# A two-layer decoder step on one core: the last squares on TensorE, two query blocks in one visit, stored keys and values claimed apart

## The chip, the core and the metric

The kernel runs on one core of one Trainium2 chip. The metric is the device time of one execution, in microseconds (us), as a median over runs. A core has TensorE (PE; its weight loads are listed apart as PEld), VectorE (DVE), ScalarE (ACT), GpSimd (POOL) and SyncE (SP), which here only issues transfers. Each engine works through its own instructions in the order of the program. TensorE's clock is granted at one of two levels, 2.4 GHz (1.00 in the tables) or 1.2 GHz (0.50).

## What is computed

One step of a two-layer trunk on 1056 tokens: 1024 of a prompt and 32 of a sample group (8 sequences of 4). All of it is fp32, with a model width of 1024. In short form:

```python
# layer 0: one projection feeds a convolution branch and a dilated attention branch
h = rms_norm(x, pre_norm[0])                 # mean of squares over the 1024 channels
a_val, a_gate, a_out, q, k, v, b_gate = split(h @ w_in_ab)      # 7 blocks of 1024
ya = swish(layer_norm(conv31(a_val * sigmoid(a_gate)))) * silu(a_out)
q, k = rope(q), rope(k)                      # 16 heads of 64
# same heads under (window, dilation) (128,1), (512,4), (2048,16), merged by their denominators
yb = merged_attention(q, k, v) * silu(b_gate)
#   sample group: its keys and values are the stored caches (2048 rows) and its own 4
x1 = x + rms_norm(concat(ya, yb) @ w_out_ab, post_norm[0])
# layer 1: gated linear recurrence, 16 heads of 128 x 128
q, f, v, g = split(rms_norm(x1, pre_norm[1]) @ w_in_c)
y = x1 + rms_norm(recurrence(q, f, v) * silu(g) @ w_out_c, post_norm[1])
```

The outputs are y, the new keys and values, the new convolution rows and the new states.

## The kernel before

**The dense stream.** Tokens lie along the free axis in three chunks of 384, 384 and 288 columns. A dense job is one block of 128 output channels: for each chunk, 8 x 3 matmuls of 128 x 128 weights in the split form (high and low halves in fp32r). There are 152 such jobs: 56 for the first projection, 16 for each output projection, 64 for layer 1. They are one long stream on TensorE, and everything else is side work.

**The order.** `Kern` is a planner that runs while the program is built. It keeps a clock per engine (`account`, with the costs in `cost` and `array`), and it writes every instruction in the order in which it decides. After each three dense matmuls it calls `sides()`, which places the next step (`Atom`) of any thread whose inputs are due by its books. A step for TensorE is placed once its inputs have been due for 300 ns (`LEAD`) and the clocks of ACT and DVE are at most 1500 ns ahead. Threads go by priority. All transfers are issued by SP, in the planner's order. The chip then follows that fixed order, and each engine waits at its next instruction for whatever is late.

**Memory.** `Arena` has 28 pages of 1056 columns, 17 halves of 512 and 8 small buffers. A thread may claim pages for what it will take (`claim`, in pages and halves); a step with a claim isn't placed until that many are free. PSUM has three buffers for the dense stream (d), four for the side work (x, taken by `px()`) and one for attention outputs (o).

**Prologue.** X is loaded as four tiles per chunk, each holding two blocks of channels side by side. ScalarE squares them. VectorE adds tile 1 to tile 0, 3 to 2, 2 to 0, and folds the two halves of tile 0 into one (`add`, `fold`). `stat(c)` multiplies the result with a constant matrix (`self.ones`), which sums over partitions, and `rstd_of` makes the factors of the norm. The evacuations of the first dense job are placed once the statistic of chunk 2 is due. `turn(c)` scales the tables of the rotation on POOL.

**Attention of the prompt.** There are eight pairs of heads, each a thread (`attention`). The prompt is cut into eight query blocks of 128. `qk(i)` writes the scores of block i for both heads in the 64 x 32 tiling of TensorE: 8 matmuls on the near keys and, from block 2 on, 8 on the far keys. VectorE adds the mask and takes the extremum, and ScalarE takes the exponential. `tr(i)` and `far(i)` turn the probabilities, and `pv(i)` and `far_pv` multiply them with the values. Such a group of matmuls, placed between dense ones, is called a visit here. In the trace one fp32 matmul is two records.

**Stored-key rounds.** For the sample group there are 16 rounds (8 pairs, two groups g of four sequences), each a thread made by `dec_thread` from `dec_round`. A round issues four loads of keys (kc) and four of values (vc), builds the query block, writes the scores (`qk`), turns the probabilities (`tr1`, `tr2`), multiplies them with the values (`pv`) and stores its part (`out`). The rounds run beside the last 16 jobs of the first projection and the first of the output projection.

Of the kernel before, what the change touches and what calls it, by code (L numbers as in the profile page):

```python
# [177 lines left out]
class Kern:  # L178
# [481 lines left out]
    def prologue(self):  # L660
# [50 lines left out]
        def add(c, k, m, eng):  # L711
            x, y = X[c, k], X[c, m]
            do(lambda: eng.tensor_tensor(x.f, x.f, y.f, op=OP.add), ("s", c, k), ("s", c, k), ("s", c, m))
            y.free()
# [6 lines left out]
        def stat(c):  # L721
            def f():
                w = CW[c]
                x = X[c, 0]
                p = self.px()
                nc.tensor.matmul(p[:, :w], self.ones.f, x[:, :w], start=True, stop=True)
                self.rstd_of(self.R[:, C0[c]:C0[c] + w], p[:, :w])
                x.free()
            return f
# [44 lines left out]
        for c in range(3):  # L774
            for k in range(n):
                square(c, k, True)
            add(c, 0, 1, V)
            add(c, 2, 3, V)
            add(c, 0, 2, V)
            fold(c)  # L780
        for c in range(3):
            self.fin["pro", c] = at["s", c, 0]
            self.spawn(f"pro{c}", 0.1 * c, [Atom(stat(c), "pe", [("pro", c)], ("r0", c)),
                                            Atom(turn(c), "pool", None, ("cs", c))])
# [170 lines left out]
    def attention(self, pr):  # L955
# [7 lines left out]
        def qk(i):  # L963
            def f():
                if i == 0:
                    S["den"] = A.alloc(16)
                    S["o"] = A.alloc(T)
                nf, nn = width(i)
                W = nf + nn
                kc = slice(128 * (i + 1) - nn, 128 * (i + 1))  # L970
                hs = [slice(64 * h, 64 * h + 64) for h in range(2)]
                ss = []
                for h in range(2):
                    P[i, h] = A.alloc(W + 8)
                    ss.append(self.px())
                q, k = S["q"], S["k"]
                for a, b, ks in ((nf, W, kc), (0, nf, None)):
                    for r in range(4):
                        for h in range(2):
                            if b > a:  # L980
                                nc.tensor.matmul(ss[h][32 * r:32 * r + 32, a:b],
                                                 q[hs[h], 128 * i + 32 * r:128 * i + 32 * r + 32],
                                                 k[hs[h], ks or slice(r, 128 * i, 4)], start=True, stop=True,
                                                 skip_group_check=True, tile_position=(64 * h, 32 * r))
                t = self.cur
                for h in range(2):
                    e = P[i, h]
                    m = e[:, W:W + 1]
                    self.resume(t)
                    nc.vector.tensor_tensor_reduce(e[:, :W], ss[h][:, :W], self.mask[:, NMASK - W:NMASK],  # L990
                                                   op0=OP.add, op1=OP.min, scale=-0.125, scalar=1e30, accum_out=m)
                    nc.scalar.activation(e[:, :W], e[:, :W], AF.Exp, scale=-1.0, bias=m,
                                         accum_out=S["den"][:, h * 8 + i:h * 8 + i + 1])
            return f
# [81 lines left out]
        for i in range(9):  # L1076
            if i < 8:
                atoms.append(Atom(qk(i), "pe", [K("pv", i - 2)] if i > 1 else [("ko", pr)], K("qk", i),
                                  (2, 7) if i == 0 else None))
# [310 lines left out]
    def dec_thread(self, pr):  # L1390
        nc, A = self.nc, self.A
        KN = NCK + NS
        for g in range(2):
            self.spawn(f"dec{pr}.{g}", 3 + 0.01 * (2 * pr + g), self.dec_round(pr, g, {}), ("att", pr))
# [18 lines left out]

    def dec_round(self, pr, g, R):
        nc, A = self.nc, self.A
        KN = NCK + NS

        def load(name, j):
            def f():
                b = A.alloc(NCK)  # L1420
                R.setdefault(name, []).append(b)
                nc.sync.dma_start(b.f, self.io[name][pr, 4 * g + j])
            return f
# [11 lines left out]
        def qk():  # L1435
# [22 lines left out]
            nc.scalar.activation(e[:, :KN], e[:, :KN], AF.Exp, scale=-1.0, bias=x[:, 2:3], accum_out=x[:, 3:4])  # L1458
            nc.vector.reciprocal(x[:, 4:5], x[:, 3:4])
# [38 lines left out]
        def out():  # L1498
# [3 lines left out]
            for h in range(2):  # L1502
# [6 lines left out]
        lds = [Atom(load(n, j), "sp", [], K(k) if j == 3 else None, (8, 0) if (k, j) == ("k", 0) else None, True)  # L1509
               for n, k in (("kc", "k"), ("vc", "v")) for j in range(4)]  # L1510
        return lds[:1] + [Atom(blk, "pool", [], K("q"))] + lds[1:] + ([Atom(lambda: self.dec_v(pr), "pe", [])] if g == 0 else []) + [
                Atom(qk, "pe", [K("k"), K("q")], K("s"), (6, 0)), Atom(tr1, "pe", [K("s")], K("t1")),
                Atom(tr2, "pe", [K("s")], K("t2")), Atom(pv, "pe", [K("t1"), K("t2"), K("v")], K("pv")),
                Atom(out, "pe", None, K("o"))]
# [1121 lines left out]
```

## Time and profile before

| | |
|---|---|
| median of 3 runs | 2325.9 us (2324.64 to 2326.06) |
| profiled execution | 2328.87 us |
| its span, first to last instruction | 2327.0 us, mean granted clock 0.994 |
| PE and PEld busy | 2262.7 and 2116.6 us (97% and 91%) |
| DVE, ACT, POOL busy | 1601.6, 1026.3, 1026.5 us (69%, 44%, 44%) |
| moved by DMA | 271.60 MB, 117 GB/s over the span |

All times in the profile are counted from the start of the span. Nearly every instruction is issued through one helper, so all rows carry its line, L158, and they are told apart by the names of the tiles: d, x and o are PSUM buffers, c are constants and the split X, b is any buffer of the arena, and kc, vc, wab and so on are arrays in device memory. A row "out<-in" gives what an instruction writes and reads, with the forms of both. The ends of matmuls are modelled, so what a group of them took is read from its start to the start of the next row.

### The profile page before, as it was taken

What the parts mean: (1) busy time and instruction counts of PE and PEld (TensorE: products, weight loads), DVE (VectorE), ACT (ScalarE), POOL (GpSimd) and SP (SyncE); (2) the same over time, 40 slices, a digit from 0 to 9 for tenths busy, and PEclk for the clock granted to TensorE, in tenths of its full rate; (3) what the DMA queues carried; (4) which work ended last, traced back from release to release, by engine and by line L of the source; (5) the groups of instructions that cost most, each with busy time, mean ns of one, the idle gap of its engine ahead of it and who ended that gap; (6) DMA issues with size and microseconds to landing.
All of it is one profiled execution on the core that took longest, in us unless ns stands there. A gap on an engine that the chain in (4) does not pass through costs nothing.

```text
span 2327.0 us, 42803 instructions
## 1 busy us (share of the span) xinstructions
PE 2262.7 (97%) x17415; PEld 2116.6 (91%) x17415; DVE 1601.6 (69%) x2477; ACT 1026.3 (44%) x1862; POOL 1026.5 (44%) x678
## 2 busy tenths in 40 slices
PE   7999999999999999999999999999999999999997
PEld 7988888888887788899989999999999999998997
DVE  7999899898996557533865666666766666667436
ACT  5454444444444322332564444444454444454422
POOL 4554474645555423543633333333333333344435
PEclk9999999999999999999999999999999999999999
DMA  5121231221247977962541111111121111132426
GB/s 172 49 86 32 76 87 41 78 76 49 70 155 266 342 282 271 331 225 78 187 149 65 65 65 65 65 65 65 47 85 65 65 65 65 65 123 72 168 88 200
DMA packets 118173, 271.60 MB, mean 117 GB/s; under 512 B 32336, under 2 KB 59472, under 8 KB 117968
## 3 DMA queue, kind: packets, MB, share of 16 engines
q1 hardware_dynamic: 117968, 268.78, 33.9%
q8 instruction: 139, 2.28, 0.4%
q14 instruction: 66, 0.54, 0.1%
HBM read 215.00 MB, written 53.73 MB: 115 GB/s over the span
## 4 chain that ended last, share of the span: by engine, by line
PE 68%; DVE 14%; issue 7%; DMA 4%; POOL 3%; ACT 3%; SPq 0%; POOLq 0%; DVEq 0%; ACTq 0%
PE d L158 38%; PE x L158 29%; DVE b L158 14%; POOL b L158 3%; ACT b L158 2%; DMA b<-kc 1%; PE o L158 1%; DMA b<-ybd 1%; DVE c L158 1%; DMA b<-wab 1%; SPq L158 0%; DMA b<-rd 0%; DMA b<-vc 0%; POOL c L158 0%; DMA b<-x 0%
## 5 line engine op out<-in xcount | busy, mean ns | idle before, releaser
L158 PE MATMUL d<-c,b 128*128 128x384 f32 (+1 forms) x7920 | 1387.7, 329 | 8.4 <-ACT b L158 7.8
L158 PEld LDWEIGHTS d<-c,b 128*128 128x128 f32 x7920 | 1279.3, 189 | 53.8 <-issue 40.3
L158 POOL TENSOR_TENSOR b<-b,b 128x1024 fp32r<-128x1024 f32 (+5 forms) x401 | 827.3, 2076 | 835.0 <-ACT b L158 637.3
L158 ACT ACTIVATE b<-b 128x384 f32<-128x384 f32 (+15 forms) x647 | 358.2, 569 | 804.7 <-DVE b L158 786.4
L158 PE MATMUL x<-c,b 128*128 128x384 f32 (+3 forms) x3616 | 583.8, 312 | 11.8 <-ACT b L158 5.3
L158 PEld LDWEIGHTS x<-c,b 128*128 128x128 f32 (+1 forms) x3616 | 540.1, 175 | 30.1 <-ACT b L158 8.8
L158 DVE TENSOR_TENSOR b<-b,b 128x384 f32<-128x384 f32 (+13 forms) x296 | 316.9, 1081 | 89.1 <-ACT b L158 71.4
L158 DVE SCALAR_TENSOR_TENSOR b<-b,c,b 128x1024 f32<-128x1024 f32 (+1 forms) x218 | 364.3, 1671 | 9.9 <-ACT b L158 7.5
L158 PE MATMUL x<-b,b 128*32 128x128 f32 (+12 forms) x4552 | 286.7, 338 | 6.4 <-DVE b L158 5.7
L158 DVE SCALAR_TENSOR_TENSOR b<-b,b 128x384 f32<-128x384 f32 (+3 forms) x216 | 188.3, 877 | 105.7 <-ACT b L158 101.4
L158 PEld LDWEIGHTS x<-b,b 64*32 64x32 f32 (+3 forms) x4552 | 205.6, 128 | 57.6 <-issue 37.4
L158 ACT CAST b<-b 128x1024 fp32r<-128x1024 f32 (+3 forms) x264 | 224.6, 861 | 18.8 <-DMA b<-woc 5.2
L158 DVE TENSOR_TENSOR b<-d,b 128x384 f32<-128x384 f32 (+3 forms) x278 | 139.8, 509 | 127.8 <-PE d L158 124.3
L158 DVE TENSOR_TENSOR b<-x,b 128x288 f32<-128x288 f32 (+3 forms) x164 | 83.3, 508 | 136.2 <-PE x L158 121.7
L158 POOL TENSOR_SCALAR b<-b 128x32 f32<-128x32 f32 x40 | 27.3, 682 | 295.2 <-DVE b L158 269.6
L158 ACT COPY b<-x 128x512 f32<-128x512 f32 (+4 forms) x175 | 85.4, 496 | 159.1 <-PE x L158 143.4
L158 DVE COPY b<-x 128x512 f32<-128x512 f32 (+7 forms) x219 | 102.5, 479 | 73.6 <-PE x L158 66.6
L158 ACT COPY b<-d 32x384 f32<-32x384 f32 (+2 forms) x212 | 94.8, 447 | 114.7 <-DVE b L158 77.9
L158 ACT ACTIVATE b<-b,c 128x512 f32<-128x512 f32 (+2 forms) x114 | 96.3, 869 | 3.6 <-DVE b L158 1.2
L158 DVE CUSTOM_DVE_ANT_0 b<-x,b 128x128 f32<-128x128 f32 (+8 forms) x144 | 72.0, 533 | 34.4 <-PE x L158 32.7
L158 POOL COPY b<-b 128x32 f32<-128x32 f32 (+1 forms) x105 | 59.1, 573 | 69.0 <-DVE b L158 67.3
L158 DVE TENSOR_TENSOR b<-b,x 128x128 f32<-128x128 f32 x144 | 53.9, 374 | 36.9 <-PE x L158 32.7
(61 smaller groups left out, 968.2 us busy)
## 6 DMA issues: line engine op xcount, KB each, us to landing
b<-wc SPq DMA_DIRECT2D x64, 512.0 KB, 4.2
b<-wab SPq DMA_DIRECT2D x56, 512.0 KB, 5.8
b<-kc SPq DMA_DIRECT2D x64, 448.0 KB, 6.3
b<-vc SPq DMA_DIRECT2D x64, 448.0 KB, 8.3
b<-woa SPq DMA_DIRECT2D x32, 512.0 KB, 3.7
b<-woc SPq DMA_DIRECT2D x32, 512.0 KB, 4.2
b<-yd SPq DMA_DIRECT2D x16, 528.0 KB, 6.2
ybd<-b SPq DMA_DIRECT2D x16, 512.0 KB, 3.0
```

Of the source, the lines that this page charges most:

```text
L158: r = f(*a, **k)
```

## The change

It has three parts. In the prologue, chunk 2 keeps its two sums apart: VectorE no longer adds tile 2 to tile 0 nor folds, and `stat(2)` accumulates four matmuls (two halves of two tiles) where it had one. In the attention of each pair, the scores of blocks 0 and 1 are written in one step, `qk(0, 1)`, into the same two PSUM buffers side by side; the reductions and exponentials follow block by block, and each block is marked as due by itself. In the stored-key rounds, the thread of a round claims 5 pages and loads the keys; a second thread (`dec_values`), which becomes ready when the keys are due, claims 4 and loads the values; the claim at the scores is 2 where it was 6; and the reciprocal of the denominators is a step of its own (`rec`).

```diff
--- before.py
+++ after.py
@@ -721,11 +721,14 @@
         def stat(c):
             def f():
                 w = CW[c]
-                x = X[c, 0]
                 p = self.px()
-                nc.tensor.matmul(p[:, :w], self.ones.f, x[:, :w], start=True, stop=True)
+                xs = [X[c, k] for k in ((0, 2) if c == 2 else (0,))]
+                parts = [x[:, a:a + w] for x in xs for a in ((0, w) if c == 2 else (0,))]
+                for n, x in enumerate(parts):
+                    nc.tensor.matmul(p[:, :w], self.ones.f, x, start=(n == 0), stop=(n == len(parts) - 1))
                 self.rstd_of(self.R[:, C0[c]:C0[c] + w], p[:, :w])
-                x.free()
+                for x in xs:
+                    x.free()
             return f
 
         def turn(c):
@@ -776,10 +779,11 @@
                 square(c, k, True)
             add(c, 0, 1, V)
             add(c, 2, 3, V)
-            add(c, 0, 2, V)
-            fold(c)
+            if c < 2:
+                add(c, 0, 2, V)
+                fold(c)
         for c in range(3):
-            self.fin["pro", c] = at["s", c, 0]
+            self.fin["pro", c] = max(at["s", c, 0], at["s", c, 2] if c == 2 else 0)
             self.spawn(f"pro{c}", 0.1 * c, [Atom(stat(c), "pe", [("pro", c)], ("r0", c)),
                                             Atom(turn(c), "pool", None, ("cs", c))])
 
@@ -960,37 +964,44 @@
         def width(i):
             return 32 * i * (i > 1), 128 * min(i + 1, 2)
 
-        def qk(i):
-            def f():
-                if i == 0:
+        def qk(*blocks):
+
+            def f():
+                if blocks[0] == 0:
                     S["den"] = A.alloc(16)
                     S["o"] = A.alloc(T)
-                nf, nn = width(i)
-                W = nf + nn
-                kc = slice(128 * (i + 1) - nn, 128 * (i + 1))
                 hs = [slice(64 * h, 64 * h + 64) for h in range(2)]
-                ss = []
-                for h in range(2):
-                    P[i, h] = A.alloc(W + 8)
-                    ss.append(self.px())
                 q, k = S["q"], S["k"]
-                for a, b, ks in ((nf, W, kc), (0, nf, None)):
-                    for r in range(4):
-                        for h in range(2):
-                            if b > a:
-                                nc.tensor.matmul(ss[h][32 * r:32 * r + 32, a:b],
-                                                 q[hs[h], 128 * i + 32 * r:128 * i + 32 * r + 32],
-                                                 k[hs[h], ks or slice(r, 128 * i, 4)], start=True, stop=True,
-                                                 skip_group_check=True, tile_position=(64 * h, 32 * r))
+                ss = [self.px() for h in range(2)]
+                off, at = {}, 0
+                for i in blocks:
+                    off[i] = at
+                    at += sum(width(i))
+                for i in blocks:
+                    nf, nn = width(i)
+                    W = nf + nn
+                    kc = slice(128 * (i + 1) - nn, 128 * (i + 1))
+                    for a, b, ks in ((nf, W, kc), (0, nf, None)):
+                        for r in range(4):
+                            for h in range(2):
+                                if b > a:
+                                    nc.tensor.matmul(ss[h][32 * r:32 * r + 32, off[i] + a:off[i] + b],
+                                                     q[hs[h], 128 * i + 32 * r:128 * i + 32 * r + 32],
+                                                     k[hs[h], ks or slice(r, 128 * i, 4)], start=True, stop=True,
+                                                     skip_group_check=True, tile_position=(64 * h, 32 * r))
                 t = self.cur
-                for h in range(2):
-                    e = P[i, h]
-                    m = e[:, W:W + 1]
-                    self.resume(t)
-                    nc.vector.tensor_tensor_reduce(e[:, :W], ss[h][:, :W], self.mask[:, NMASK - W:NMASK],
-                                                   op0=OP.add, op1=OP.min, scale=-0.125, scalar=1e30, accum_out=m)
-                    nc.scalar.activation(e[:, :W], e[:, :W], AF.Exp, scale=-1.0, bias=m,
-                                         accum_out=S["den"][:, h * 8 + i:h * 8 + i + 1])
+                for i in blocks:
+                    W = sum(width(i))
+                    for h in range(2):
+                        e = P[i, h] = A.alloc(W + 8)
+                        m = e[:, W:W + 1]
+                        self.resume(t)
+                        nc.vector.tensor_tensor_reduce(e[:, :W], ss[h][:, off[i]:off[i] + W],
+                                                       self.mask[:, NMASK - W:NMASK],
+                                                       op0=OP.add, op1=OP.min, scale=-0.125, scalar=1e30, accum_out=m)
+                        nc.scalar.activation(e[:, :W], e[:, :W], AF.Exp, scale=-1.0, bias=m,
+                                             accum_out=S["den"][:, h * 8 + i:h * 8 + i + 1])
+                    self.fin["qk", pr, i] = max(self.end, self.cur)
             return f
 
         def tr(i):
@@ -1074,9 +1085,9 @@
         atoms = [Atom(store, "sp", [("rk", pr, c) for c in range(3)] + [("rq", pr, c) for c in range(3)], ("ko", pr))]
         K = lambda n, i: (n, pr, i)
         for i in range(9):
-            if i < 8:
-                atoms.append(Atom(qk(i), "pe", [K("pv", i - 2)] if i > 1 else [("ko", pr)], K("qk", i),
-                                  (2, 7) if i == 0 else None))
+            if i < 8 and i != 1:
+                atoms.append(Atom(qk(*((i,) if i else (0, 1))), "pe", [K("pv", i - 2)] if i else [("ko", pr)], None,
+                                  None if i else (2, 7)))
             if i:
                 t = i - 1
                 atoms.append(Atom(tr(t), "pe", [K("qk", t)], K("tr", t)))
@@ -1389,9 +1400,11 @@
 
     def dec_thread(self, pr):
         nc, A = self.nc, self.A
-        KN = NCK + NS
         for g in range(2):
-            self.spawn(f"dec{pr}.{g}", 3 + 0.01 * (2 * pr + g), self.dec_round(pr, g, {}), ("att", pr))
+            R = {}
+            prio = 3 + 0.01 * (2 * pr + g)
+            self.spawn(f"dec{pr}.{g}", prio, self.dec_round(pr, g, R), ("att", pr))
+            self.spawn(f"decv{pr}.{g}", prio + 0.005, self.dec_values(pr, g, R), ("dec", pr, g, "k"))
 
         def gate():
             y = self.qs[:, pr * NS:pr * NS + NS]
@@ -1411,16 +1424,23 @@
         v = self.decv[pr] = A.alloc(128)
         nc.vector.tensor_copy(v[0:32, :], p[0:32, 0:128])
 
+    def dec_load(self, name, pr, g, R):
+        def load(j):
+            def f():
+                b = self.A.alloc(NCK)
+                R.setdefault(name, []).append(b)
+                self.nc.sync.dma_start(b.f, self.io[name][pr, 4 * g + j])
+            return f
+
+        return [load(j) for j in range(4)]
+
+    def dec_values(self, pr, g, R):
+        return [Atom(f, "sp", [], ("dec", pr, g, "v") if j == 3 else None, None if j else (4, 0), True)
+                for j, f in enumerate(self.dec_load("vc", pr, g, R))]
+
     def dec_round(self, pr, g, R):
         nc, A = self.nc, self.A
         KN = NCK + NS
-
-        def load(name, j):
-            def f():
-                b = A.alloc(NCK)
-                R.setdefault(name, []).append(b)
-                nc.sync.dma_start(b.f, self.io[name][pr, 4 * g + j])
-            return f
 
         def blk():
             R["qb"] = A.alloc(128)
@@ -1456,6 +1476,9 @@
                 nc.vector.tensor_tensor_reduce(e[:, a:b], s, m, op0=OP.add, op1=OP.min, scale=-0.125,
                                                scalar=x[:, n - 1:n] if n else 1e30, accum_out=x[:, n:n + 1])
             nc.scalar.activation(e[:, :KN], e[:, :KN], AF.Exp, scale=-1.0, bias=x[:, 2:3], accum_out=x[:, 3:4])
+
+        def rec():
+            x = R["x"]
             nc.vector.reciprocal(x[:, 4:5], x[:, 3:4])
 
         def tr1():
@@ -1506,12 +1529,13 @@
             R["o"].free()
 
         K = lambda n: ("dec", pr, g, n)
-        lds = [Atom(load(n, j), "sp", [], K(k) if j == 3 else None, (8, 0) if (k, j) == ("k", 0) else None, True)
-               for n, k in (("kc", "k"), ("vc", "v")) for j in range(4)]
-        return lds[:1] + [Atom(blk, "pool", [], K("q"))] + lds[1:] + ([Atom(lambda: self.dec_v(pr), "pe", [])] if g == 0 else []) + [
-                Atom(qk, "pe", [K("k"), K("q")], K("s"), (6, 0)), Atom(tr1, "pe", [K("s")], K("t1")),
-                Atom(tr2, "pe", [K("s")], K("t2")), Atom(pv, "pe", [K("t1"), K("t2"), K("v")], K("pv")),
-                Atom(out, "pe", None, K("o"))]
+        lds = [Atom(f, "sp", [], K("k") if j == 3 else None, None if j else (5, 0), True)
+               for j, f in enumerate(self.dec_load("kc", pr, g, R))]
+        return (lds[:1] + [Atom(blk, "pool", [], K("q"))] + lds[1:]
+                + ([Atom(lambda: self.dec_v(pr), "pe", [])] if g == 0 else [])
+                + [Atom(qk, "pe", [K("k"), K("q")], K("s"), (2, 0)), Atom(rec, "dve"), Atom(tr1, "pe", [K("s")], K("t1")),
+                   Atom(tr2, "pe", [K("s")], K("t2")), Atom(pv, "pe", [K("t1"), K("t2"), K("v")], K("pv")),
+                   Atom(out, "pe", None, K("o"))])
 
 
     def load_hl(self, tag, c, src, dst, dep, pages=0, n=3):
```

## Rows read from the trace of the kernel before

**Rows 1.** The page: span, then busy us, share and instructions of each engine.

```profile
span 2327.0 us, 42803 instructions
...
PE 2262.7 (97%) x17415; PEld 2116.6 (91%) x17415; DVE 1601.6 (69%) x2477; ACT 1026.3 (44%) x1862; POOL 1026.5 (44%) x678
```

**Rows 2.** Timeline of PE, prologue: start, us, instruction, count [idle before, releaser].

```profile
28.95 1.45 PE L158 MATMUL x<-b,c 128*128 128x384 f32 x4
29.95 1.49 PE L158 MATMUL x<-c,b 128*128 128x384 f32 x6
35.76 1.30 PE L158 MATMUL x<-b,c 128*128 128x288 f32 x2 [4.32 <-DVE b L158]
36.44 2.54 PE L158 MATMUL x<-c,b 128*128 128x384 f32 x6
38.77 18.69 PE L158 MATMUL d<-c,b 128*128 128x288 f32 x111
```

**Rows 3.** Timeline of DVE there, from several windows: one add, three, the third, fold.

```profile
28.59 2.93 DVE L158 TENSOR_TENSOR b<-b,b 128x576 f32<-128x576 f32 x1
...
28.59 5.86 DVE L158 TENSOR_TENSOR b<-b,b 128x576 f32<-128x576 f32 x3
...
33.02 1.43 DVE L158 TENSOR_TENSOR b<-b,b 128x576 f32<-128x576 f32 x1
...
34.48 1.13 DVE L158 TENSOR_TENSOR b<-b 128x288 f32<-128x288 f32 x1
```

**Rows 4.** Stretches: us, busy PE PEld DVE ACT POOL, PEclk, DMA, GB/s.

```profile
31.40:34.60 3.20, 0.04 (x1) 0.00 (x0) 3.13 (x4) 0.53 (x2) 3.20 (x3) 1.00 0.00 0
34.60:35.80 1.20, 0.04 (x1) 0.07 (x1) 1.20 (x2) 0.00 (x0) 1.20 (x2) 0.52 0.00 0
35.80:41.50 5.70, 5.70 (x20) 5.41 (x21) 1.31 (x3) 3.25 (x5) 2.23 (x3) 0.50 0.01 1
```

**Rows 5.** Timeline of PE, dense stream without side work.

```profile
1077.75 4.38 PE L158 MATMUL x<-c,b 128*128 128x384 f32 x24
1081.97 4.38 PE L158 MATMUL d<-c,b 128*128 128x384 f32 x24
```

**Rows 6.** Timeline of PE: four fp32 matmuls of 288 columns after layer 0.

```profile
1202.08 2.10 PE L158 MATMUL x<-b,c 128*128 128x288 f32 x8
1203.81 0.55 PE L158 MATMUL d<-c,b 128*128 128x384 f32 x1
```

**Rows 7.** Timeline of PE, first pair: scores of blocks 0 and 1.

```profile
93.91 0.45 PE L158 MATMUL x<-b,b 64*32 64x128 f32 x16
94.29 0.79 PE L158 MATMUL d<-c,b 128*128 128x384 f32 x3
95.01 0.66 PE L158 MATMUL x<-b,b 64*32 64x256 f32 x16
95.60 1.65 PE L158 MATMUL d<-c,b 128*128 128x384 f32 x8
```

**Rows 8.** Groups of PE, 661.2 to 1008.5; waits, 660 to 1010 (us, times, longest).

```profile
L158 PE MATMUL x<-c,b 128*128 128x128 f32 x174 | 27.1, 277 | 6.3 <-ACT b L158 5.1 <-DVE b L158 1.1
...
PEld x L158 <- DMA b<-kc: 2.9, 3, 1.0
```

**Rows 9.** The page, DMA issues: count, KB each, median us to landing.

```profile
b<-kc SPq DMA_DIRECT2D x64, 448.0 KB, 6.3
b<-vc SPq DMA_DIRECT2D x64, 448.0 KB, 8.3
```

**Rows 10.** Timeline of PE, one stored-key round: its scores and its value product.

```profile
822.37 1.77 PE L158 MATMUL x<-b,b 128*32 128x512 f32 x24
...
830.38 2.09 PE L158 MATMUL x<-b,b 128*32 128x128 f32 x64
```

**Rows 11.** PE timeline and stretch, late in layer 1: another long wait.

```profile
2116.99 1.08 PE L158 MATMUL x<-b,b 128*32 128x128 f32 x16 [2.28 <-DVE b L158]
...
2117.40:2120.80 3.40, 3.40 (x32) 3.00 (x22) 1.96 (x3) 0.96 (x2) 0.00 (x0) 0.59 0.00 0
```

## The prediction

> **What bounds the kernel now.** I read the page first: TensorE holds the span, busy for 97% of it, with its weight loads at 91%; VectorE follows at 69% [rows 1]. So an edit counts by what it takes from TensorE's row: instructions, changes of tiling, waits, or time at the low clock. The page can't say which, so the second view was TensorE's timeline over the prologue. It holds the longest single wait that the change touches: 4.32 us before the third statistic (35.76), ended by VectorE [rows 2]. The third view, VectorE's timeline of that stretch, says why: after the squares, three adds of 576 columns run to 34.45 (the last starts at 33.02 and takes 1.43) and the fold to 34.48 + 1.13 = 35.61; the statistic starts 0.15 later [rows 3]. The fourth view is the table by stretches: the granted clock is still 1.00 until 34.60, falls within the wait, and stays at 0.50 (1.2 of 2.4 GHz) until about 41.5 [rows 4]. The reader should see two losses there, the wait and the half pace behind it. The pace itself: six matmuls take 36.44 to 38.77 = 2.33 us [rows 2], where 24 of the same shape take 4.22 at full clock, 0.176 each, so 1.05 for six [rows 5].
>
> **The change part by part. First, the squares of the last chunk.** VectorE loses the third add and the fold, 1.43 + 1.13 = 2.56 us [rows 3]. TensorE gets three more fp32 matmuls of 288 columns on the constant matrix. Four of that shape take 1202.08 to 1203.81, 0.43 each [rows 6], so 1.30 more. Two of the four read only the first sum, complete at 28.59 + 2.93 = 31.52 [rows 3], and run while VectorE makes the second; that sum is complete at 33.02, the last two start at 33.17 and end at 34.03, where the statistic ended at 36.44 before [rows 2, 3]. It is 2.41 earlier.
>
> Not all of that is gain. TensorE runs in program order, and the planner puts the statistic where, by its own books, the input has been ready for 0.3 us (LEAD). It books the two dropped operations at 750 and 450 ns less 83 each, 1.03 us, which is six dense matmuls; I take it that six now stand behind the statistic rather than ahead, 1.05 us. At full clock: between 36.44 and 41.5 the old kernel did, at half pace, 2.53 us worth of full-pace work. The new one does those 2.53 and the six moved, 1.05, from 34.03 on, and is through at 37.61: 3.9 us ahead. Bounds: if the six are not moved, 4.9; if the clock falls all the same, 34.03 + 2 x 3.58 = 41.19, a gain of 0.3, and a loss of 0.6 if the last two matmuls run at half too. I take 3.9, because what is left of the wait is two short pieces (about 30.4 to 31.5 and 32.4 to 33.2, 1.9 us in all) and the clock was whole through 3.2 us of the old one [rows 4]. The work that follows has its cover: VectorE scales the first evacuation right after its last add, 2.6 earlier too, so no accumulator is short for the moved matmuls.
>
> The Trainium skill, FP8 and Floating Point Precision, TensorE Precision Notes, says that a true fp32 product passes the array four times, which speaks against giving sums to TensorE. The three matmuls by that rule, as an estimate, are 4 x 288 columns at 2.4 GHz, 0.48 each and 1.44 together, and the total below would be 0.1 smaller.
>
> **Second, two query blocks in one visit.** For each of eight pairs the blocks 0 and 1 are two visits, with three dense matmuls between. Block 0 costs TensorE 93.91 to 94.29 = 0.38, block 1 costs 95.01 to 95.60 = 0.59 [rows 7]. The three between take 0.72 where 3 x 0.176 = 0.53 would do, so entering the small tiling costs 0.19. 128 columns more cost 0.21, which leaves 0.17 as the fixed part of a visit; one visit of 384 columns should cost 0.80 against 0.97. Saved: 0.17 + 0.19 = 0.36 a pair, 2.9 us in eight. Bounds: nothing, if the second visit overlapped with something that I can't see; 0.19 a pair, 1.5, if the fixed part stays; 4.6, if block 0 hides behind block 1 altogether (0.38 + 0.19). I take 2.9, since each term is a difference of starts on the bounding engine. VectorE and ScalarE do the same reductions and exponentials as before. The first one starts up to 0.4 later; block 0's transpose waits for it, and dense matmuls fill TensorE meanwhile. Without that cover it would cost those 0.4 a pair, and the gain would be gone. Score buffers: two of four are held until all four reductions are done, where four were used.
>
> **Third, the stored-key rounds.** Sixteen rounds between 661 and 1009 us. TensorE's instructions stay the same; pages, order on the SP queue and one VectorE operation change. Before, a round claims 8 pages for keys and values together and issues eight loads in a row. Now a round claims 5, issues four key loads, and a second thread claims 4 and issues the values only when the keys are booked as landed. So the four value issues pass whatever SP has in between (weights, reloads, stores), and stand just ahead of, or at, the score visit. The reciprocal is now a step of its own, so that VectorE's next instructions no longer queue behind one that waits for the exponential; what waits for the reciprocal is only the last scaling of the round.
>
> What it can win is what TensorE waits for there: 6.3 us before transposes and read-outs, 5.1 of it for ScalarE, and 2.9 us before weight loads, for keys, in three waits [rows 8]. All gone, that is 9.2. What it can lose: values now land late. They took 8.3 us from issue, keys 6.3 [rows 9]; a typical round has its score visit at 822.37 and its value visit at 830.38, 8.0 later [rows 10]. Issued at the score visit, the values land about when TensorE wants them. The keys already live under that rule, and three waits of sixteen came of it at 0.97 each; every value visit waiting so would cost 15.5. I take zero between these ends: 2.9 lost for values (the keys' own row), and as much won back from the 6.3, of which the waits for ScalarE are untouched in kind. Finishing the rounds earlier wins nothing by itself: the dense work behind them stands on TensorE either way.
>
> **Sum.** 3.9 + 2.9 + 0 = 6.8 us. The profiled execution took 2328.87, its span 2327.0 and 1.9 outside; it lies 3.0 above the median of the runs. From the median, 2325.9 - 6.8 = 2319.1.
>
> **The rivals.**
> The clock falls anyway. For it: a wait of 2.28 us, about as long as what I leave, had a granted clock of 0.59 right after it [rows 11]. Against: mine is broken by two matmuls. Then the first part gives 0.3, and the sum is 3.2: 2322.7. The Trainium skill, TensorE: Matmul & The Clock Gate, part 1, says that the watch on TensorE's activity runs free of the kernel, so that where a wait falls decides too. No row here shows that, and it would make a run to run difference of this case.
>
> Values come late, the case on the other side. The place is the value visit of each round. At 0.97 each, 15.5 more, the time is 2334.6; it turns slower than before by a measurable amount once the waits exceed 6.8 + 4.65 = 11.5, or 0.72 a round. For it: 8.0 against 8.3 [rows 9, 10]. Against: the planner books the landing too and moves the visit.
>
> The visits were no cost, or the order shifts and gives all back: the planner's books move from 30 us on, and the waits of pairs and heads fall elsewhere. Then nothing is won: 2325.9.
>
> The rounds gain. Pages held for less time let the waits of [rows 8] vanish: 9.2 more, 2309.9. Against: none of those rows names a page.
>
> **How the numbers follow.** A measurement of this kernel tells about 0.2%, 4.65 us, from no change. Forecast 0.50, its own range 2315 to 2322; clock falls 0.22; values late 0.10; given back 0.10; rounds gain 0.08. Faster: 0.43 of the forecast, 0.03 of the clock case, 0.08 of the last, 0.54. Slower: 0.09 of late values and 0.01 of the reshuffle, 0.10. The rest, 0.36, is no change, to which the clock case belongs almost whole. The range 2312.5 to 2327 leaves out late values and most of the last case, 0.17; it holds both ends of the first two parts (from 0.9 gained to 9.5, with the third part at zero).
>
> **What will show it.** First part: eight records for the third statistic, the wait ahead of it in pieces under 2 us, and clock 1.00 between 35.8 and 41.5; a 0.50 there proves the rival. Second: in each pair the 128 and 256 column scores stand next to each other with no dense row between, and 0.80 from the first score to the next dense matmul. Third: waits of weight loads for values (none now) against those for keys. The forecast is wrong if values show more than 5 us in that view, or if the 3.9 us gained at 41.5 are not there at 300.

## The result and the profile after

The changed kernel takes 2303.24 us (median of 4 runs, 2302.36 to 2303.92), against 2325.98 for the kernel before in the same measurement (4 runs, 2324.64 to 2328.17). The ratio is 0.9897, with a 95% interval of 0.9885 to 0.9908: 22.7 us are gone. I had forecast 2319.1 and a range down to 2312.5, so the sign was right and the size was three times too small. The profiled execution has a span of 2301.3 us, 25.7 less than before [rows 1].

The page first: the span, the engines' row, and two rows of its DMA issues.

```profile
span 2301.3 us, 42896 instructions
...
PE 2253.1 (98%) x17421; PEld 2114.1 (92%) x17421; DVE 1613.5 (70%) x2477; ACT 1021.7 (44%) x1860; POOL 1041.9 (45%) x678
...
b<-kc SPq DMA_DIRECT2D x64, 448.0 KB, 7.4
b<-vc SPq DMA_DIRECT2D x64, 448.0 KB, 7.1
```

TensorE's busy time fell by 9.6 us only; the rest of the 25.7 is time in which it stood. Keys and values have changed places: 7.4 and 7.1 us to landing, where it was 6.3 and 8.3 [rows 9].

TensorE's timeline over the prologue, the counterpart of [rows 2]:

```profile
29.42 0.91 PE L158 MATMUL x<-b,c 128*128 128x384 f32 x2 [0.26 <-DVE b L158]
29.88 0.98 PE L158 MATMUL x<-c,b 128*128 128x384 f32 x3
32.35 1.21 PE L158 MATMUL x<-b,c 128*128 128x288 f32 x4 [1.49 <-DVE b L158]
33.73 1.24 PE L158 MATMUL x<-b,c 128*128 128x288 f32 x4 [0.17 <-DVE b L158]
34.59 3.00 PE L158 MATMUL x<-c,b 128*128 128x384 f32 x15
```

The statistic is eight records in two halves, and the wait of 4.32 us has become 1.49 + 0.17. The stretches there (us, busy PE, granted clock, DMA share, GB/s) say that the clock stayed at its upper level, where it had been halved [rows 4]:

```profile
31.00:34.60 3.60, 2.08 (x9) 1.00 0.00 0
34.60:35.80 1.20, 1.20 (x8) 1.00 0.00 0
35.80:41.50 5.70, 5.70 (x41) 1.00 0.00 0
```

In the last of them 41 records ran, 20 before. The first pair of heads, again on TensorE's timeline, the counterpart of [rows 7]:

```profile
92.32 0.88 PE L158 MATMUL x<-b,b 64*32 64x128 f32 x32
93.13 1.84 PE L158 MATMUL d<-c,b 128*128 128x384 f32 x9
```

One visit, no dense row inside it (the row is named by its first form), and 0.81 us from its start to the next dense matmul.

**Where the 25.7 us came from.** I cut both traces at the same places of the dense stream: the starts of its 97th, 289th, 2881st, 5185th and last matmul, read from TensorE's timeline. The first stretch holds the statistic, the second (jobs 4 to 39) the pairs, the third (jobs 40 to 71) the stored-key rounds, and the fourth all that follows. "Idle" is the sum of TensorE's idle times there.

| stretch | before, us (idle) | after, us (idle) | gain |
|---|---|---|---|
| statistic, #97 to #289 | 41.16 | 38.15 | 3.0 |
| pairs, to #2881 | 605.50 (13.8) | 594.18 (6.0) | 11.3 |
| rounds, to #5185 | 493.27 (9.1) | 484.56 (2.8) | 8.7 |
| rest, to the last | 1144.78 | 1142.29 | 2.5 |

The 0.2 that is missing lies ahead of the first cut and behind the last. Each stretch is that of one profiled execution; the executions of one kernel lie up to 11 us apart in total (the kernel before, 25 times: 2322.3 to 2332.9). So the prologue gave about what it should, the pairs four times as much, and the rounds, put at nothing, gave 8.7. In the rest the change does nothing by itself: TensorE spent 6.8 us of it at the low clock, 13.7 before, and half of that difference is 3.4. Without the rest the stretches give 23.0, near the 22.7 of the medians.

The waits of TensorE from 99 to 705 us, which is the pairs and the first of the rounds, before and after (us in total, times, longest):

```profile
PE o L158 <- DVE b L158: 9.2, 12, 1.6
PE x L158 <- DVE b L158: 3.2, 5, 1.3
PE x L158 <- ACT b L158: 1.7, 3, 1.2
```

```profile
PE o L158 <- DVE b L158: 4.1, 13, 0.8
PE x L158 <- DVE b L158: 1.2, 5, 0.4
PE x L158 <- ACT b L158: 0.4, 1, 0.4
```

And the rounds after: the group of PE that answers to [rows 8] (647 to 1000 us), then the two longest waits from 645 to 1000 us.

```profile
L158 PE MATMUL x<-c,b 128*128 128x128 f32 x174 | 26.5, 275 | 0.4 <-ACT b L158 0.3
```

```profile
PE d L158 <- POOL b L158: 1.0, 1, 1.0
PE x L158 <- DMA b<-vc: 0.7, 1, 0.7
```

The 6.3 us ahead of transposes are 0.4, and values were late once, by 0.7.

### The profile page after: what moved, and what is told of

Same layout as the page of the kernel before. It is cut to its first block, busy times and chain, and to the rows that moved or that the text cites. A ratio compares the mean times of both kernels' runs of the same rounds, so it can differ in the third digit from the quotient of the medians.

```text
span 2301.3 us, 42896 instructions
## 1 busy us (share of the span) xinstructions
PE 2253.1 (98%) x17421; PEld 2114.1 (92%) x17421; DVE 1613.5 (70%) x2477; ACT 1021.7 (44%) x1860; POOL 1041.9 (45%) x678
## 3 DMA queue, kind: packets, MB, share of 16 engines
q8 instruction: 139, 2.28, 0.4%
## 4 chain that ended last, share of the span: by engine, by line
PE 60%; issue 4%; DVE 4%; POOL 2%; DMA 1%; ACT 1%; SPq 0%; POOLq 0%; ACTq 0%; DVEq 0%
PE d L158 32%; PE x L158 28%; DVE b L158 4%; POOL b L158 2%; ACT b L158 1%; DMA b<-kc 0%; PE o L158 0%; SPq L158 0%; DMA rd<-b 0%; POOL c L158 0%; DMA b<-woc 0%; DMA b<-x 0%; DMA b<-od 0%; DMA b<-rd 0%; DVE c L158 0%
## 5 line engine op out<-in xcount | busy, mean ns | idle before, releaser
L158 POOL TENSOR_TENSOR b<-b,b 128x512 f32<-128x512 f32 (+5 forms) x402 | 836.6, 2093 | 833.8 <-ACT b L158 615.6
L158 DVE TENSOR_TENSOR b<-b,b 128x384 f32<-128x384 f32 (+13 forms) x294 | 331.6, 1138 | 88.5 <-ACT b L158 70.9
L158 DVE TENSOR_TENSOR b<-x,b 128x384 f32<-128x384 f32 (+3 forms) x160 | 81.1, 507 | 130.7 <-PE x L158 116.1
L158 ACT COPY b<-x 128x512 f32<-128x512 f32 (+5 forms) x178 | 85.0, 489 | 140.8 <-PE x L158 133.1
L158 POOL COPY b<-b 128x32 f32<-128x32 f32 (+1 forms) x105 | 65.5, 634 | 62.7 <-DVE b L158 60.9
L158 DVE CUSTOM_DVE_ANT_0 b<-x,b 128x512 f32<-128x512 f32 (+8 forms) x144 | 71.4, 532 | 26.6 <-PE x L158 26.4
```

Source lines behind the costliest of these rows:

```text
L158: r = f(*a, **k)
```

## The experiments

The edits move the order of everything behind them, since the planner decides by its clocks; so each is cut at the same places as above, and the stretches are told beside the total. A new order of the same work is called a draw here. Ratios are to the kernel before in the same measurement.

| kernel | median us | ratio, 95% interval | statistic | pairs | rounds | rest |
|---|---|---|---|---|---|---|
| e1 squares alone | 2327.45 | 1.0001 [0.9991, 1.0010] | 39.41 | 611.6 | 490.7 | 1143.8 |
| e2 joint scores alone | 2321.37 | 0.9973 [0.9963, 0.9982] | 41.15 | 596.9 | 494.8 | 1145.0 |
| e3 rounds alone | 2328.92 | 0.9997 [0.9988, 1.0007] | 40.96 | 605.2 | 492.1 | 1145.9 |
| e4 squares and scores | 2316.11 | 0.9948 [0.9931, 0.9965] | 38.00 | 594.3 | 493.4 | 1145.4 |
| n1 before, shift 300 | 2331.00 | 1.0012 [1.0002, 1.0022] | 41.13 | 608.2 | 493.4 | 1145.4 |
| n2 before, shift 700 | 2337.17 | 1.0038 [1.0026, 1.0051] | 41.04 | 608.5 | 500.9 | 1143.5 |
| n3 after, shift 300 | 2321.28 | 0.9975 [0.9965, 0.9984] | 39.38 | 604.9 | 493.0 | 1144.6 |
| n4 after, shift 700 | 2313.85 | 0.9938 [0.9921, 0.9955] | 38.04 | 595.3 | 491.6 | 1145.9 |
| m1 before, fewer products | 2330.53 | 1.0006 [0.9996, 1.0016] | 40.38 | 614.5 | 490.1 | 1144.2 |
| m2 after, fewer products | 2327.14 | 1.0005 [0.9996, 1.0015] | 37.34 | 612.6 | 488.6 | 1144.0 |
| d1 after, late shift 150 | 2309.93 | 0.9925 [0.9908, 0.9941] | 38.15 | 594.4 | 490.3 | 1143.2 |
| d2 e4, late shift 150 | 2319.68 | 0.9967 [0.9954, 0.9979] | 38.14 | 594.9 | 497.9 | 1145.8 |
| d3 after, shift at 44 | 2306.04 | 0.9905 [0.9889, 0.9922] | 38.16 | 594.2 | 485.4 | 1144.4 |
| d4 e4, shift at 44 | 2308.93 | 0.9918 [0.9901, 0.9934] | 38.13 | 594.7 | 487.8 | 1145.3 |
| d5 after, shift at 47 | 2305.71 | 0.9903 [0.9886, 0.9919] | 38.16 | 594.3 | 485.1 | 1144.7 |
| d6 e4, shift at 47 | 2316.36 | 0.9949 [0.9932, 0.9965] | 37.34 | 594.2 | 495.5 | 1146.4 |
| r1 e4 and claims apart | 2310.50 | 0.9919 [0.9901, 0.9937] | 38.00 | 594.9 | 489.9 | 1144.6 |
| r2 e4 and own reciprocal | 2315.40 | 0.9940 [0.9924, 0.9957] | 38.11 | 594.1 | 493.3 | 1145.5 |

**The parts alone.** The theories were that each part owns what it gains, or that a new order deals the waits anew. Each kernel is the one before with the changed lines of that part: e1 has those of `stat`, `add` and `fold`, e2 those of `qk(*blocks)`, e3 those of `dec_thread`, `dec_load`, `dec_values` and `dec_round`.

```diff
+            if c < 2:                                   # e1
+                add(c, 0, 2, V)
+                fold(c)
...
+            if i < 8 and i != 1:                        # e2
+                atoms.append(Atom(qk(*((i,) if i else (0, 1))), "pe", ...
...
+            self.spawn(f"decv{pr}.{g}", prio + 0.005, self.dec_values(pr, g, R), ("dec", pr, g, "k"))   # e3
```

> The kernel before with the prologue's part alone (four matmuls in the third statistic). Theory 'own gains': each part has its own, so the dense stream is some 3 us ahead at 60 us (3.3 counted from the first dense matmul, as in the changed kernel) and keeps that: 2323. Rival 'reshuffle': the waits of TensorE for VectorE in the attention of the pairs (13.8 us before, 6.0 after) hang on how the order happens to fall, and any shift of the order redraws them; then this kernel too differs from before by several us between 68 and 660 us, in either direction: 2316 to 2330, and its waits there are neither 13.8 nor 6.0.

> The kernel before with the joint score visit alone. 'Own gains': 2.9 us from eight visits saved, and the waits of the pairs fall from 13.8 to about 6 because of the joint visit: 10 to 11 us in all, 2315, and pairs at an even period of some 83 us. 'Reshuffle': 2.9 us for certain, the waits anywhere between 4 and 18: 2313 to 2327, no even period.

> The kernel before with the stored-key rounds' part alone. Up to 660 us the order is that of before, so nothing changes there. 'Own gains': TensorE's waits between 670 and 1010 fall from 9.1 to about 3 and the 3.3 us inside one score visit for keys go, 8 us in all: 2318. 'Reshuffle': between 2 lost and 9 won, 2317 to 2328.

> The changed kernel without the stored-key rounds' part. Up to 660 us its order is that of the changed kernel: 14 us ahead of before there. 'Own gains': 2312, the rest (8 us) is the rounds' part. 'Reshuffle': the rounds of before, begun at another point of the stream, get other waits, 2306 to 2316.

By the ratios the parts alone sum to about 7 us (6.3 of it the joint scores), by the medians to 3, and together they give 22.7: no simple sum. None of the three came to its 'own gains' figure (2323, 2315 and 2318). The stretches say why. The squares gain 1.75 in their own stretch, and the pairs behind them lose 6.1, with a single wait of 4.4 for a weight's split on POOL, toward the end of which the granted clock fell to 0.50, from 168.5 to 175.3 us (both come again in n3). The joint scores gain 8.6 in the pairs alone and 11.2 beside the squares. The rounds' part alone gives 1.2.

**A shift without meaning.** To see what a new order does by itself, the planner's clock of TensorE is moved forward once ahead of the pairs and once ahead of the rounds; no instruction changes, only the order.

```diff
         for job in jobs:
+            self.njob = getattr(self, "njob", 0) + 1
+            if self.njob in (6, 42):
+                c["pe"] += 300
```

> The kernel before, same work, with the planner's own TensorE clock set 0.3 us forward twice (at the sixth dense job and at the 42nd, where the rounds begin), so that the order of the side work is drawn anew. 'Reshuffle' (the gain beyond 6 us is luck of the order): waits of TensorE in the pairs between 5 and 18 us and in the rounds between 3 and 12, total anywhere in 2310 to 2335. 'Own gains' (joint visit and split rounds take the waits away): waits stay near 13.8 and 9, total within 5 us of before.

> The kernel before with a shift of 0.7 us at the same two jobs, another draw of the order. 'Reshuffle': anywhere in 2310 to 2335. 'Own gains': waits near 13.8 and 9, total within 5 us of before.

> The changed kernel with the 0.3 us shift at the same two jobs. 'Reshuffle': the 23 us fall back to between 5 and 20, as the waits in the pairs (6.0) and in the rounds (2.8) go up to what other draws give: 2306 to 2321. 'Own gains': the planner of the changed kernel finds its even order again, waits near 6 and 3, 2301 to 2306.

> The changed kernel with a shift of 0.7 us at the same two jobs, another draw of the order. 'Reshuffle': 2306 to 2321. 'Own gains': waits near 6 and 3, 2301 to 2306.

The shift moves the kernel before by 3 to 10 us and the changed one by 11 to 18, all upwards. Both kernels are thus good draws of their own order. Under the same shift the difference between them is 9.7 us (300) and 23.3 (700), where it was 22.7. With the joint scores the pairs take 594.3, 595.3, 596.9 and 604.9 in four different orders, without them 605.5, 608.2, 608.5 and 611.6. The means are 597.9 and 608.4.

**What TensorE waits for in the pairs.** In a pair the longest waits stand before the value products (`pv`), for VectorE. Here is one of the kernel before, with rows from the timelines of the three engines that have a part in it:

```profile
520.93 4.61 DVE L158 SCALAR_TENSOR_TENSOR b<-b,c,b 128x1024 f32<-128x1024 f32 x2
...
526.28 0.68 DVE L158 COPY b<-x 128x512 f32<-128x512 f32 x1
...
521.59 2.86 POOL L158 TENSOR_TENSOR b<-b,b 128x1024 fp32r<-128x1024 f32 x1 [7.08 <-ACT b L158]
...
527.01 0.66 PE L158 MATMUL o<-b,b 128*64 128x128 f32 x8 [1.38 <-DVE b L158]
```

Two products of the convolution branch take 4.61 us, since POOL splits a weight in between; the copy that TensorE waits for stands behind them. The same place after:

```profile
508.69 2.89 POOL L158 TENSOR_TENSOR b<-b,b 128x1024 fp32r<-128x1024 f32 x1 [1.85 <-ACT b L158]
...
513.05 2.59 DVE L158 SCALAR_TENSOR_TENSOR b<-b,c,b 128x1024 f32<-128x1024 f32 x2
...
517.11 0.66 PE L158 MATMUL o<-b,b 128*64 128x128 f32 x8 [0.17 <-DVE b L158]
```

The split began 4.4 us ahead of the two products, they take 2.59, and the wait is 0.17. (It stretched another product there, to 2.32 us, and no instruction of TensorE waited behind that one.) In the whole trace of before, the 69 products of this form with nothing of GpSimd beside them took 1.18 to 1.29 us, and the 135 beside one of its two-input operations 1.93 in the mean, 3.50 at most. The Trainium skill, SBUF — State Buffer, "SBUF: two separate sides", says that VectorE and GpSimd share a port pair which one instruction holds to its end. The 4.61 against 2.59 agree with it.

To test the cause, two kernels leave out 25 of the 26 products that VectorE does for each channel block of the convolution (its output is then only the first product's), without and with the change:

```diff
-                else:
-                    y = S["y"][:, :T]
-                    nc.vector.scalar_tensor_tensor(y, u[:, w:w + T], cw, y, op0=OP.mult, op1=OP.add)
```

> The kernel before without 25 of the 26 products of the convolution that VectorE adds per channel block (200 instructions of 1.3 to 2.3 us left out). Theory 'taps in the way': TensorE waits in the pairs because reductions and copies stand behind such products on VectorE, which POOL's weight splits stretch; without them the waits of the pairs fall from 13.8 to under 3 us and the stage from job 4 to job 40 from 605.5 to about 594. Rival 'the visits themselves' (waits come of the order of steps in a pair): waits stay above 8.

> The changed kernel without the same products. 'Taps in the way': with the cause gone, the joint visit is worth its instructions alone, so this kernel and the one before without products differ in that stage by 2.5 us (seven pairs at 0.36), where with the products they differ by 11.3. Rival: they still differ by 8 or more.

The waits before the value products of the first seven pairs, 9.9 us before and 4.1 after, went to 0.00 in both, so the products are their cause, as far as an edit can tell that also draws a new order. The two differ in the pairs by 1.9 us where the full kernels differ by 11.3. But the announced fall of all waits to under 3 us didn't come: TensorE was idle there for 10.8 and 14.0 us, and the stretches got longer (614.5 and 612.6). TensorE's waits up to 682 us are now (m1, then m2):

```profile
PE x L158 <- DVE b L158: 4.0, 6, 0.8
PE x L158 <- ACT b L158: 3.5, 7, 0.5
PE x L158 <- POOL b L158: 2.8, 1, 2.8
```

```profile
PE x L158 <- ACT b L158: 10.9, 7, 1.7
PE x L158 <- POOL b L158: 2.7, 1, 2.7
```

In m1 score visits wait for VectorE and transposes for ScalarE's exponentials, in m2 transposes wait for nearly all of it, and 13.7 and 17.1 us of the stretch ran at the low clock. Less work on VectorE was no gain.

**Is the rounds' part worth 8.7, or a draw?** e4 and the changed kernel share their work up to the rounds; both are shifted late, at the same place by the same amount, in three ways.

```diff
+            self.njob = getattr(self, "njob", 0) + 1
+            if self.njob == 42:                 # d1, d2; at 44 by 400: d3, d4; at 47 by 800: d5, d6
+                c["pe"] += 150
```

> The changed kernel with the planner's TensorE clock 0.15 us forward at dense job 42 alone, so the order is the changed kernel's up to 660 us and only the rounds are drawn anew. If the rounds' part has a gain of its own of 8 us, the stage from job 40 to job 58 takes 323 to 328 us here (324.6 in the changed kernel); if most of that was a lucky draw, 329 to 335.

> Squares and joint visit, rounds as before, the same shift of 0.15 us at job 42. The stage of the rounds took 333.4 without the shift; if draws scatter by some 4 us, 329 to 338; if the rounds' part has its own gain, this stays 6 or more above the run with it.

> The changed kernel with 400 ns added once to the planner's clock of TensorE at job 44 of the dense stream, four jobs into the stretch of the stored-key rounds (jobs 40 to 71): the same work up to there, a new draw of the order behind it. Measured is the stretch from job 40 to job 72. 'Lucky draw': the changed kernel's 484.6 us there is no property of the new rounds, so 490 to 493 and a total near 2309. 'Own gain of the rounds': 484 to 487 again, total near 2304.

> The same shift with the first two parts only (rounds as before the change). 'Own gain of about 3 us, the rest luck': 494 to 496 in the stretch, three above its partner. 'Own gain of 8': 8 above its partner. 'No own gain': the two within 1.5 us of each other, or this one lower.

> The changed kernel with 800 ns added at job 47: one more draw. 'Lucky draw': 490 to 493 in the stretch. 'Own gain': 484 to 487.

> The first two parts only with 800 ns added at job 47. 'Own gain of about 3': 494 to 496; 'of 8': 8 above its partner; 'none': within 1.5 us of its partner or lower.

d1 and d2 were announced for jobs 40 to 57. There they took 329.8 and 327.0, so the kernel with the part was the slower one; but in d2 the last round runs on behind job 57, with 196 records of side work behind it where d1 has 2, and so jobs 40 to 71 are compared, which hold the same work in both.

Kernel against kernel, the part shortens its stretch by 8.9 (no shift), 7.6, 2.4 and 10.4 us, 7.3 in the mean, and by 1.2 where the other two parts are missing (e3). After e1 to e4 and d1 I had held the 484.6 of the changed kernel for a lucky draw. d3 and d5, at 485.4 and 485.1, are against that. n3 and n4, which reach the rounds by another order, are for it: 493.0 and 491.6 with the part. Over the table, the seven kernels with the whole part take 488.9 in the mean (484.6 to 493.0) and the nine with none of it, m1 and m2 apart, 494.2 (487.8 to 500.9). So the part has a gain of its own, some 5 to 7 us, and the 8.7 is a good draw of it.

**Which half of it?** The part separates the claims of keys and values, and it makes the reciprocal a step of its own. VectorE's reciprocals of the rounds offered themselves as the cause. Their groups (count, busy, mean ns, then VectorE's idle time before them), before, after and in r2:

```profile
L158 DVE RECIPROCAL b<-b 128x1 f32<-128x1 f32 x16 | 2.6, 164 | 19.3 <-ACT b L158 19.2
```

```profile
L158 DVE RECIPROCAL b<-b 128x1 f32<-128x1 f32 x16 | 2.5, 156 | 1.3 <-ACT b L158 1.3
```

```profile
L158 DVE RECIPROCAL b<-b 128x1 f32<-128x1 f32 x16 | 2.5, 157 | 3.3 <-ACT b L158 3.1
```

```diff
-                + [Atom(qk, "pe", [K("k"), K("q")], K("s"), (2, 0)), Atom(rec, "dve"), Atom(tr1, ...      # r1, from the changed kernel;
+                + [Atom(qk, "pe", [K("k"), K("q")], K("s"), (2, 0)), Atom(tr1, ...                        # the reciprocal back in qk
...
-                Atom(qk, "pe", [K("k"), K("q")], K("s"), (6, 0)), Atom(tr1, ...                            # r2, from e4
+                Atom(qk, "pe", [K("k"), K("q")], K("s"), (6, 0)), Atom(rec, "dve"), Atom(tr1, ...
```

> The changed kernel with the reciprocal put back into the score step of the rounds; keys and values stay apart. 'The reciprocal': VectorE's wait of about 19 us in 17 reciprocals comes back, the stretch from job 40 to job 72 takes 491 to 498 and TensorE waits there 7 us or more, a total near 2312. 'The claims': the stretch stays at 485 to 490, total near 2305.

> The first two parts and, of the third, only the reciprocal as a step of its own; keys and values are claimed together as before. 'The reciprocal': VectorE's wait at the reciprocals is below 6 us, the stretch takes 484 to 490, total near 2305. 'The claims': 493 to 498 in the stretch, total near 2314. Of the reciprocal's effect the values' late landing is no part here, so waits for loads should be those of before.

r2 takes 16 us of idle time from VectorE, and its stretch is 493.3, that of e4: nothing speaks for the reciprocal alone. The claims alone give 3.5 of the 8.9, with 6.8 us at the low clock in that draw, and TensorE's idle time is still 6.3. Both are single draws, and e4's four orders lie between 487.8 and 497.9, so this is a hint and no more. What the claims move can be read from the starts of the visits: from the n-th score visit to the n-th value visit it is 9.3 us before, 8.8 in e4 and 9.2 in r2 (medians of 16), but 11.4 in r1, 12.5 in d3 and 14.1 in the changed kernel. The round is stretched, and its transposes can stand where the exponentials are done. But the distance alone doesn't make the gain: it is 13.3 in e3 and d1 and 12.9 in n3 and n4, whose stretches took 490.3 to 493.0. What those kernels wait for is not one thing: 3.9 and 3.1 us for keys in n3 and n4, and some 2 us each for ScalarE, POOL and VectorE in e3 and d1. How the claims make the gain, whether it needs both halves, and whether r1 drew badly stay open.

## Why the prediction fell short

**The squares: right, and a little too large.** Predicted 3.9, measured 3.0. The next dense matmul behind the statistic starts 2.28 us earlier against the 97th (predicted 2.41). The half pace that was saved is 2.51: the 174 matmuls from the 115th to the 289th took 31.60 before and 29.09 after (predicted 2.53). The mis-sized term is the moved matmuls. I took six, 1.05 us, and nine stand behind the statistic now, 1.78 us, the first of them 0.39. 2.28 + 2.51 - 1.78 = 3.0. My reading of [rows 6] was part of it: 0.43 a matmul stops at the start of the next row, while the fp32 records start 0.242 apart, 0.48 a matmul, and the dense matmul behind them takes 0.39 where the next take 0.17. The 0.48 that the prediction gave as an estimate was the better price. The rival "the clock falls anyway" wasn't this run, but it is real: see the last section. There (e1) the part still gained 1.75 in its stretch, not 0.3.

**The joint visit: its own price right, the larger effect not in the sum.** 0.81 us against 0.80 predicted. Over seven pairs the score visits cost 52.16 where they cost 53.46, and the dense matmuls between, idle time left out, 444.35 where they cost 445.58: 0.36 a pair, as forecast. The rest of the 11.3 is 7.8 of idle time and 1.1 in the transposes (42.17 to 41.09). What failed is the step that says "VectorE and ScalarE do the same reductions and exponentials as before", and leaves TensorE's waits for them out. The stretch held 13.8 us of idle time, 12.4 of it for VectorE in the waits shown above; the view of all waits had these rows too, but I used it for the rounds alone, so nothing of it came into the sum or the range. With one visit fewer the pairs follow each other faster in every order. Three pairs, from the first value product of pair 3 to that of pair 6 (counted from 0), take 253.2 us in the kernel before (352.2 to 605.4) and 253.0 to 253.3 in e1, n1 and n2. In the changed kernel they take 250.2 (344.9 to 595.1), and 249.0, 250.8 and 249.2 in e2, n3 and n4. In the mean that is 84.4 and 83.3 a pair, 1.1 less, of which the visit is 0.36 and most of the rest the waits. Why one visit fewer brings VectorE's copies in time was not tested by itself. That isn't all of the stretch, though: n3 drew 604.9 with it, by waits in its first pairs.

**The rounds: zero was wrong, and the rival that priced it was mine.** The step that failed is "I take zero between these ends", with its reason "of which the waits for ScalarE are untouched in kind". They went from 6.3 to 0.4 [rows 8]. The upper bound of 9.2 was the size of it, and I gave that rival 0.08, since none of its rows named a page. Pages need not be named by a wait: the planner places a step when they are free, and so they set what is ready when TensorE comes to it. That 9.2 and 8.7 lie so close is luck: the keys' waits, which the bound counted too, did not vanish (2.9 before, 2.8 after), and of the 8.7 only 6.2 is idle time of TensorE, while the dense matmuls gave 2.5 (381.67 to 379.18). The 0.4 is a good draw too: the waits ahead of transposes are 0.0 to 2.4 us in the seven kernels with the part, 1.1 to 7.1 in the nine without.

**Values late: refuted.** One wait of 0.7 us in sixteen rounds, 1.7 in all at most in the redrawn kernels with all three parts (d5), and 3.2 in r1, where the reciprocal is back in the score step. On the weight loads, where 5 us was to be the sign, it is 1.0, 2.7 and 3.8. Values took 7.1 us to land, and the value visit moved away from the score visit.

**Given back by the order: half right.** I priced it as a loss of all the gain. The order does move every stretch by several us, but in the three orders in which both kernels were run the difference is 22.7, 9.7 and 23.3 us, 18.6 in the mean. (d1, d3 and d5 are no further draws of the whole: they share the changed kernel's order up to the rounds.) The range was too narrow by what an order can move: it had bounds for each instruction and none for that.

## What to carry to other kernels

Where a program's order is planned, an edit's worth is its instructions and the waits that it redeals: read all waits of the bounding engine in the stretch that is touched, and let the range hold them. Before an edit's gain is believed or a part's loss is taken for its own, shift the planner by an amount that means nothing, and compare several orders of each kernel, cut at the same places of the work. Idle time that goes away on an engine that isn't the bound need not be worth anything: the 16 us at the reciprocals left the stretch at 493.3.

## What was not expected of the hardware

The same wait left the clock whole in the profiled execution of one kernel and halved it in that of another. After a wait of 1.49 us ahead of the statistic the granted clock was 1.00; in e1, with 1.51 us and the same prologue, the stretches read (us, busy PE, granted clock, DMA share, GB/s)

```profile
31.00:34.60 3.60, 2.84 (x7) 0.64 0.00 0
34.60:35.80 1.20, 1.20 (x5) 0.67 0.00 0
```

and so it was in n3. It cost 1.26 us (39.41 against 38.15). The Trainium skill, TensorE: Matmul & The Clock Gate, part 1, says that the watch on TensorE runs free of the kernel; these runs fit it: the instructions are the same and the waits as long, and only the time differs at which they fall (30.25 to 31.76 us in e1, 30.86 to 32.35 in the changed kernel). That this decides is not shown.
